# An encoder layer on one core: the first Fourier half by a written order, with its arithmetic off GpSimd and one tile in another buffer

## The chip, the cores and the metric

The kernel runs on one core of a Trainium2 chip. The core has a matrix engine (TensorE, PE in the profile, with PEld for its weight loads), a vector engine (VectorE, DVE), a scalar engine (ScalarE, ACT), a general engine (GpSimd, POOL) and a queue that mostly issues transfers (SyncE, SP). The metric is the device time of one execution in microseconds; less is better. Where runs are compared, the median of several executions is used.

## The reference

Two sequences of 1024 rows by 1024 channels (the prompt, b = 0, and the sample, b = 1) go through the same layer. Cut to what matters:

```
xn = rmsnorm(x, g_pre);  p = xn @ w_in          # 8 sections of 1024 columns
fv, fg, hv, hg, mg = split(p)
fz  = real(fft over the sequence and over groups of 256 channels of fv)
y_f = (fz * silu(fg)) @ w_fourier_out
hv  = short_conv(hv, w_short);  v, x1, x2 = split(hv)
kf  = rfft of filters made by a small network (two sines, one exponential decay)
z   = v;  for gate in (x1, x2): z = gate * long_conv(z, kf[n])     # FFT of length 2048
y_h = (z * silu(hg)) @ w_hyena_out
out = (sigmoid * y_f + sigmoid * y_h) @ w_out
y   = x + rmsnorm(out, g_post)
```

Everything is float32 in and out. Products are done on numbers split into a rounded high part and a remainder (h and l), three products for each: h by h, h by l, l by h. `split` is a rounding copy on ScalarE and a subtraction elsewhere.

## The kernel before, in words

Four stages follow one another: the Fourier branch (`phase_fourier`, to about 262 us), the filters' spectra together with some of the gate projections (the first loop of `phase_main`, to about 690 us), the long convolutions with their projections (`branches`), and the output products (`phase_tail`).

In the Fourier stage each sequence is transposed to channels by rows, scaled by `g_pre` and folded: row a is added to and subtracted from row 1024 - a, so that an even part (e = 0) and an odd part (e = 1) of half the length remain (`eo`, split to `eh` and `el`). The weights of the section `fv` are folded in the same manner (`wes` and `wos`, split to `we` and `wo`), in two halves of the channel groups. The products of the folded rows and folded weights are the sums `pfv[e, m]`, with m = 0 to 3: eight sums over eight blocks k of 128 channels. `keep` splits them to `ee` and `oo`; `fourier_half` transforms them along the sequence (`stage`: `pse`, `pso`) and along the channels (`pP`, `pQ`) and stores the result. Beside the sums there is a small product for the middle row, `pfx`, from `x5`.

The first sequence's first weight half is done by `first_half`, which works on the eight row blocks in two halves h (blocks 0, 7, 1, 6 and blocks 2, 5, 3, 4) so that work can begin when four blocks have been loaded. `scale_rows` squares the four blocks on ScalarE, gets the inverse root by a bit trick and three Newton steps of three small VectorE operations each (`rstd`), and scales the blocks, two on each engine. `two_tiles` takes two channel blocks (a pair kp): eight transposes into PSUM (`tpx`), two scaled copies to `xg` on ScalarE, a store of each to DRAM (`d_x`), two folds on VectorE, a rounding on ScalarE, a remainder on VectorE. `two_weights` loads and folds the weights of a pair; the remainder of `wo` is GpSimd's in all pairs but the first. All four pairs of h = 0 are done first, with four sums open in PSUM, then those four are kept, then come the four pairs of h = 1 with another four sums.

`hidden(0)` is the first layer of the filter network: one product, range reduction in `sin_of` on VectorE, a sine on ScalarE, a store. In later Fourier work GpSimd folds the odd part in `xtile` (the second sequence) and does one fold and one remainder for each block in `weights`.

No order is written out by hand in this stage: the framework schedules each engine's instructions by program priority in a simulated timeline, with a few edges (`issue_after`) that hold one instruction behind another on its engine. Buffers of one tag in a pool share a number of slots; a tile takes a free one, and waits if there is none.

In `filter_spectrum` the folded taps are added and subtracted to `xp` (tag `q`, two slots) and `xm` (tag `u`, one slot), then go through `butterfly` (`bs`, `b`, split to `bh` and `bl`) to the products `pXf`. The tag `u` is also that of `v`, the emptied first projection of the first branch step (`conv`, section 1). The tag `q` also holds `hid`, the network's output, which all filters' taps read. The projections (`pin`) have two PSUM pairs.

Of the kernel before, what the change touches and what calls it, by code (L numbers as in the profile page):

```python
# [9 lines left out]
F32 = mybir.dt.float32  # L10
# [6 lines left out]
P = 128  # L17
D = 1024
# [4 lines left out]
BANDS = 16  # L23

# [136 lines left out]
class K:  # L161
# [96 lines left out]
    def sin_of(self, y, k, out, src_ps, f, b):  # L258
# [12 lines left out]
        pi = 3.1415925  # L271
        nc.vector.tensor_scalar(y, y, pi, -pi, op0=ALU.min, op1=ALU.max)
        nc.scalar.activation(out, y, AF.Sin)

    def hidden(self, layer, px, pf):


        nc, a = self.nc, self.a
        h = px.tile([P, 512], F32, tag="eo", name=f"hd_{layer}", bufs=2)
        z = px.tile([P, L], F32, tag="x", name="hd_z", bufs=3)[:, 0:512]  # L280
        if layer == 0:
            w = pf.tile([P, P], F32, tag="sst", name="hd_w", bufs=1)[0:66]
            self.hfb = px.tile([P, 4], F32, name="hd_fb", bufs=1)
            z = z[0:66]
# [3 lines left out]
            y, k = [pf.tile([P, 512], F32, tag=f"{t}p0", name=f"s{t}", bufs=1 + (t == "p")) for t in "qp"]  # L288
# [7 lines left out]
        nc.tensor.matmul(p, w, z, start=True, stop=True)  # L296
        self.sin_of(y, k, h, p, self.hfb[:, 2 * layer:2 * layer + 1], self.hfb[:, 2 * layer + 1:2 * layer + 2])
        nc.sync.dma_start(self.d_h if layer else self.d_h1, h)
# [33 lines left out]
    def scale_rows(self, h, px, ss, rs):  # L332

        nc = self.nc
        q = slice(4 * h, 4 * h + 4)
        for j, m in enumerate(self.ROWS[h]):
            sq = px.tile([P, D], F32, tag="xg", name="sq", bufs=2)
            nc.scalar.activation(sq, self.xs[m], AF.Square, accum_out=ss[:, 4 * h + j:4 * h + j + 1])
        self.rstd(px, rs[:, q], ss[:, q], 4)
        for j, m in enumerate(self.ROWS[h]):  # L340
            s = rs[:, 4 * h + j:4 * h + j + 1]
            if j % 2:
                nc.scalar.mul(self.xs[m], self.xs[m], s)
            else:
                self.scaled = nc.vector.tensor_scalar(self.xs[m], self.xs[m], s, None, op0=MUL)

    def two_tiles(self, h, kp, px, fo):


        nc = self.nc  # L350
        ks = slice(2 * kp, 2 * kp + 2)
        xg = px.tile([P, 2, 514], F32, tag="xg", name=f"xg0_{h}{kp}", bufs=2)
        self.cleared = nc.gpsimd.memset(xg[:, :, 512 + h:514], 0.0)
        if h:
            nc.scalar.copy(xg[:, :, 512:513], fo["r6"][:, ks].unsqueeze(2))
        for j in range(2):
            k = 2 * kp + j
            tp = self.psum("T", 2, "tpx")
            for q, m in enumerate(sorted(self.ROWS[h])):
                nc.tensor.transpose(tp[:, q * P:(q + 1) * P], self.xs[m][:, k * P:(k + 1) * P], self.ident)  # L360
            nc.scalar.activation(xg[:, j, 0:512], tp, AF.Copy, scale=self.gpre[:, k:k + 1])
            d = self.d_x[0][k].rearrange("p (a b) -> p a b", b=256)
            self.stored = nc.sync.dma_start(d[:, 1:3] if h else d[:, 0::3], xg[:, j, 0:512].rearrange("p (a b) -> p a b", a=2))

        nc.scalar.copy(fo["r5" if h else "r6"][:, ks].unsqueeze(2), xg[:, :, 256:257])
        if h and kp == 3:
            r5 = fo["r5"].unsqueeze(2).to_broadcast([P, 8, 2])
            self.split(fo["x5"][:, :, 0:33:32], fo["x5"][:, :, 2:35:32], r5, "dve", "act")
        eo = px.tile([P, 2, 2, 2, P], F32, tag="eo", name="eo", bufs=2)
        fw = xg[:, :, 0:256].rearrange("p k (a r) -> p k r a", r=2)  # L370
        bw = xg[:, :, 512:256:-1].rearrange("p k (a r) -> p k r a", r=2)
        self.add("dve", eo[:, :, 0], fw, bw)
        self.sub("dve", eo[:, :, 1], fw, bw)
        s = slice(P * h, P * h + P)
        f = lambda t: t.rearrange("p k e r a -> p (k e r) a")
        self.split(f(fo["eh"][:, ks, :, :, s]), f(fo["el"][:, ks, :, :, s]), f(eo), "dve", "act")

    def two_weights(self, px, pw, pf, W, kp):
        nc = self.nc
        we = px.tile([P, 2, 260], F32, tag="dg", name="wes", bufs=1)  # L380
        wo = pf.tile([P, 2, 256], F32, tag=f"qp{1 - kp % 2}", name="wos", bufs=1)
        g = lambda t: t.rearrange("p (a b) -> p a b", a=2)
        for j in range(2):
            k = 2 * kp + j
            w = pw.tile([P, 2, 2, 130], F32, tag="wfv", name="wfv", bufs=2)
            nc.sync.dma_start(w.rearrange("p a b c -> p (a b c)"), self.a["w_fv"][k * P:(k + 1) * P, 0])
            self.add("dve", g(we[:, j]), w[:, :, 0], w[:, :, 1])
            self.sub("dve", g(wo[:, j]), w[:, :, 0, 0:P], w[:, :, 1, 0:P])
        for i, r in enumerate((we, wo)):
            self.split(*[p[:, 2 * kp:2 * kp + 2] for p in W[i]], r, "pool" if kp and i else "dve", "act")  # L390

    def first_half(self, pw, W, fo, px, pf, later):

        tc = self.tc
        self.xs = {}
        ss = px.tile([P, 8], F32, tag="ss", name="ss0")
        self.rs = rs = px.tile([P, 8], F32, tag="rs", name="rs0")
        self.load_rows(0, px, pf)
        self.two_weights(px, pw, pf, W, 0)
        self.load_rows(1, px, pf)  # L400
        self.scale_rows(0, px, ss, rs)
        scaled, made = self.scaled, None
        for h in range(2):
            if h:
                made = self.operands(pf)
                for e in range(2):
                    for m in (0, 2):
                        self.keep(made, e, m, p[e, m])
            p = {(e, m): self.psum(*(("X", 2) if h and e == 0 else ("mm", 4)), f"pfv{e}") for e in range(2) for m in (h, 2 + h)}
            for kp in range(4):  # L410
                if h == 0 and kp:
                    with tc.issue_after(scaled.ins):
                        self.two_weights(px, pw, pf, W, kp)
                with tc.issue_after(self.scaled.ins) if h + kp else ExitStack():
                    self.two_tiles(h, kp, px, fo)

                with tc.issue_after(self.cleared.ins):
                    for t, src in later[4 * h + kp]:
                        self.nc.gpsimd.dma_start(t, src)
                if h + kp == 0:  # L420
                    self.scale_rows(1, px, ss, rs)
                for k in (2 * kp, 2 * kp + 1):
                    for (e, m), q in p.items():
                        self.pfv(q, e, m, k, W, fo)
        return made, p

    def xtile(self, b, k, px, fo):
# [18 lines left out]
        self.sub("pool", eo[:, 1], fw, bw)  # L446
# [11 lines left out]
    def weights(self, pw, W, half, k):  # L458
# [143 lines left out]
    def phase_fourier(self):  # L602
        tc, nc, a = self.tc, self.nc, self.a
        with ExitStack() as es:
# [18 lines left out]
            for t in [fo[n] for n in ("x5", "x5t", "xx", "px")] + fo["ex"]:  # L623
                if len(t.shape) > 2:
                    t = t.rearrange("p a b -> p (a b)")
                nc.vector.tensor_scalar(t, self.ident[:, 0:1].to_broadcast(list(t.shape)), 0.0, None, op0=MUL)
# [7 lines left out]
            for b in range(NB):  # L634
# [3 lines left out]
                if b == 0:  # L638
                    self.hidden(0, px, pf)
                    W = self.open_weights(pw)  # L640
                    made, begun = self.first_half(pw, W, fo, px, pf, later)
# [5 lines left out]
                for half in ((0, 1), (1, 0))[b]:  # L647
                    if b + half not in (0, 2):
                        W = self.open_weights(pw)
                        for k in range(8):  # L650
                            self.weights(pw, W, half, k)
# [3 lines left out]
                    if (b, half) == (1, 1):  # L655
                        self.hidden(1, px, pf)
# [117 lines left out]
    def filter_spectrum(self, n, ct, T, ws):  # L774
# [7 lines left out]
        xm = ws.tile([P, 2, 4, P], F32, tag="u", name="xm", bufs=1)  # L782
# [938 lines left out]
```

## Time and profile before

| | us |
|---|---|
| median of three runs | 2364.76 (2364.63 to 2366.9) |
| the profiled execution | 2366.49 |
| its span in the trace | 2364.7 |
| TensorE busy | 2322.0 |
| VectorE busy | 1968.6 |
| ScalarE busy | 1117.0 |
| GpSimd busy | 449.8 |

A row of the busy time by stretch has the stretch, its length, then for each engine its busy time and, in brackets, its instructions (PE, PEld, DVE, ACT, POOL), then the granted clock of TensorE as a share of full speed, the busy share of the DMA engines and GB/s. A row of the timeline has the start, the duration, the engine, the line, the operation, what it writes and reads, shapes, and how many were merged (x4); in square brackets stands how long its engine was idle before it, and what ended the wait. A row of a group has the line, the engine, the operation, the tiles, the shapes and the count, then the busy time in us and the mean duration in ns, then the idle time before. Matmuls overlap: the duration of one contains its way through the array, and the step from one to the next is shorter. The helper lines are L171 (rounding copy), L177 (scalar_tensor_tensor), L181 (tensor_tensor) and L194 (matmul).

### The profile page before, as it was taken

Reading aid. Unit: us, or ns where it says so; the run is one execution under the profiler, and the core shown is the slowest. Engines: PE = TensorE matmul, PEld = TensorE weight load, DVE = VectorE, ACT = ScalarE, POOL = GpSimd, SP = SyncE. Lnnn points to the kernel's source line nnn. Section 1 sums busy time; section 2 is a strip of 40 time slices with the busy share of each in tenths; the row PEclk is TensorE's granted clock in tenths of the full one; section 3 lists DMA queues with packets and bytes.
Section 4 is the critical chain, followed back from the end, with each engine's and each line's share of the span. In section 5 each row is a group of like instructions: output and inputs, shape, how many; then the busy total and the mean of one; then the engine's idle time right before and its main releaser. Section 6 shows DMA issues by size and latency. Waiting matters only on the chain.

```text
span 2364.7 us, 36212 instructions
## 1 busy us (share of the span) xinstructions
PE 2322.0 (98%) x12784; PEld 2019.3 (85%) x12784; DVE 1968.6 (83%) x3438; ACT 1117.0 (47%) x2080; POOL 449.8 (19%) x428
## 2 busy tenths in 40 slices
PE   6999999999999999999999999999999999999998
PEld 5999888888888888888888889888888888888787
DVE  7775688888788999999989989997765578777987
ACT  6654576777753333334222223323443364557443
POOL 3342222122223343321000000112000000101311
PEclk9999999999999999999999999999999999999999
DMA  7636765554565667667465554445854678998653
GB/s 263 210 141 215 267 211 177 180 168 155 183 219 201 194 207 216 207 198 248 165 205 167 175 171 157 159 152 194 313 167 146 218 260 269 271 312 245 199 165 142
DMA packets 246207, 479.69 MB, mean 203 GB/s; under 512 B 24582, under 2 KB 82280, under 8 KB 245706
## 3 DMA queue, kind: packets, MB, share of 16 engines
q1 hardware_dynamic: 222013, 402.25, 50.9%
q0 software_dynamic: 23792, 75.11, 11.2%
q8 instruction: 100, 1.64, 0.3%
q14 instruction: 81, 0.66, 0.1%
q10 hardware_dynamic: 221, 0.04, 0.0%
HBM read 326.82 MB, written 177.73 MB: 213 GB/s over the span
## 4 chain that ended last, share of the span: by engine, by line
PE 55%; DVE 2%; DMA 1%; ACT 1%; issue 1%; POOL 0%; DVEq 0%; POOLq 0%; ACTq 0%; SPq 0%
PE pin L194 18%; PE pg L194 15%; PE pn L194 12%; PE pT L194 5%; PE pX L194 5%; PE tph L906 1%; DMA x<-d_x 1%; DMA xr<-in_x 0%; DMA d_m<-gt 0%; DMA k<-d_k 0%; DVE x L177 0%; DVE wl L181 0%; DVE t L181 0%; DVE wraw L181 0%; ACT room L171 0%
## 5 line engine op out<-in xcount | busy, mean ns | idle before, releaser
L194 PE MATMUL pin<-x,wh 128*128 128x512 f32 x2816 | 891.5, 392 | 0.6 <-DVE x L177 0.6
L194 PEld LDWEIGHTS pin<-x,wh 128*128 128x128 f32 x2816 | 525.3, 189 | 100.7 <-ACT v L873 0.8
L194 PE MATMUL pin<-x,wl 128*128 128x512 f32 x1408 | 552.1, 392 | 0.0
L181 POOL TENSOR_TENSOR wl<-wr,wh 128x512 fp32r<-128x512 f32 x128 | 224.6, 1755 | 709.7 <-ACT wh L171 682.0
L194 PEld LDWEIGHTS pin<-x,wl 128*128 128x128 f32 x1408 | 265.6, 189 | 50.0
L194 PE MATMUL pn<-room,wh 128*128 128x512 f32 x864 | 266.1, 389 | 0.0
L194 PEld LDWEIGHTS pn<-room,wh 128*128 128x128 f32 x864 | 162.1, 188 | 33.6 <-DVE gt L181 0.2
L194 PE MATMUL pn<-room,wl 128*128 128x512 f32 x432 | 168.4, 390 | 0.1
L181 DVE TENSOR_TENSOR t<-pX,k 128x1024 f32<-128x1024 f32 x128 | 156.2, 1220 | 8.7 <-PE pX L194 7.4
L194 PE MATMUL pX<-bh,cfwd 128*128 128x256 f32 x768 | 161.3, 288 | 0.0
L194 PE MATMUL pT<-cinv,yh 128*128 128x256 f32 x768 | 145.4, 284 | 0.5 <-DVE T0s L181 0.5
L171 ACT CAST wh<-wr 128x512 fp32r<-128x512 f32 x128 | 79.3, 619 | 132.7 <-PE pin L194 96.5
L171 ACT CAST bh<-b 128x512 fp32r<-128x512 f32 x144 | 88.7, 620 | 96.2 <-DVE b L181 65.5
L1362 POOL DMA_DIRECT2D d_m<-gt x32 | 27.2, 849 | 532.8 <-DVE gt L181 505.8
L194 PEld LDWEIGHTS pT<-cinv,yh 128*128 128x128 f32 x768 | 122.8, 191 | 6.5 <-issue 0.6
L194 PEld LDWEIGHTS pX<-bh,cfwd 128*128 128x128 f32 x768 | 126.3, 190 | 2.2
L171 ACT CAST yh<-y 128x512 fp32r<-128x512 f32 x96 | 59.4, 619 | 117.7 <-DVE y L181 117.7
L194 PE MATMUL pX<-bl,cfwd 128*128 128x256 f32 x384 | 109.2, 284 | 0.0
L194 PE MATMUL pT<-cinv,yl 128*128 128x256 f32 x384 | 108.9, 284 | 0.0
L181 DVE TENSOR_TENSOR bl<-b,bh 128x512 fp32r<-128x512 f32 x144 | 101.5, 709 | 3.4 <-ACT bh L171 3.3
L1105 POOL CAST mark<-x 128x1 fp32r<-128x1 f32 x30 | 22.8, 759 | 404.2 <-DVE x L177 404.0
L907 ACT COPY xt<-tph 128x512 f32<-128x512 f32 x64 | 36.9, 587 | 128.7 <-PE tph L906 128.6
(362 smaller groups left out, 5235.8 us busy)
## 6 DMA issues: line engine op xcount, KB each, us to landing
k<-d_k SPq DMA_DIRECT2D x128, 512.0 KB, 4.2
wr<-in_w_in SPq DMA_DIRECT2D x128, 256.0 KB, 3.3
d_g<-gt SPq DMA_DIRECT2D x124, 256.0 KB, 2.9
wl<-d_s SPq DMA_DIRECT2D x56, 512.0 KB, 5.5
d_k<-kt SPq DMA_DIRECT2D x128, 128.0 KB, 2.2
d_k<-kt SPq DMA_DIRECT2D x64, 256.0 KB, 2.5
g<-d_g SPq DMA_DIRECT2D x64, 256.0 KB, 5.2
r<-d_g SPq DMA_DIRECT2D x60, 256.0 KB, 6.0
```

Of the source, the lines that this page charges most:

```text
L171: self.rounded = nc.scalar.copy(h, src)
L181: return e.tensor_tensor(out, a, b, op=op)
L194: return self.nc.tensor.matmul(out, lhsT, rhs, start=start, stop=stop, skip_group_check=shared)
L906: nc.tensor.transpose(tp[:, q * P:(q + 1) * P], eo[:, e, q], self.ident)
L907: nc.scalar.copy(xt[:, e].rearrange("p a b -> p (a b)"), tp)
L1105: with tc.issue_after(nc.gpsimd.tensor_copy(mark, z[:, 0:1]).ins):
L1362: nc.gpsimd.dma_start(dst, t, accum_op=ADD)
```

## The change

There are four parts.

1. `first_half` is written out as one order. `in_order` links each instruction that it issues on TensorE, VectorE, ScalarE and SyncE behind the one before it on that engine; other instructions may still stand between. The pairs of both halves are interleaved, from (h, kp) = (0,0), (0,1), (0,2), (1,0), (1,1), (0,3), (1,2), (1,3). All eight sums are open at once: the four even ones in four banks, the four odd ones two by two in two banks. The high products of a pair are issued before those with the rows' remainder. The inverse root is a square root on ScalarE, a reciprocal and one Newton step; three of the eight squares go to VectorE; scaling is done in halves of 512 columns. The second weight pair is loaded early, into free row buffers. The remainders of `wo` are VectorE's. `keep` of m = 0 and 2 comes after the last product. Fourteen matmuls of the identity by itself stand before the first products.
2. `hidden(0)` gets twenty such matmuls behind its product, and its sine and store are issued at the end of `first_half`. The zeroing of some tiles reads `ones` (set on the core) in place of the loaded identity. The weights of the second half are held behind the remainder of (0,3) on VectorE.
3. In `xtile` and `weights` the odd fold and the remainder move from GpSimd to VectorE.
4. In the last filter, `xm` takes the tag `q` with two slots in place of `u`.

```diff
+    def in_order(self):
+        traced = self.nc.cur_bb.bb.instructions
+        last = traced[-1]
+        yield
...
+                if i.engine in prev:
+                    self.tc.add_manual_dep(i, prev[i.engine].name, ...NoSync...)
...
-        nc.scalar.activation(out, y, AF.Sin)
...
+        if layer == 0:
+            warm = self.psum("X", 2, "warm")
+            for _ in range(WARM):
+                nc.tensor.matmul(warm[:, 0:P], self.ident, self.ident, start=True, stop=True)
...
+        def norms(h):
+            q = slice(4 * h, 4 * h + 4)
+            nc.scalar.activation(root[:, q], ss[:, q], AF.Sqrt, bias=eps, scale=1.0 / D)
+            nc.vector.tensor_scalar(low[:, q], ss[:, q], -0.5 / D, -0.5 * RMS_EPS, op0=MUL, op1=ADD)
+            nc.vector.reciprocal(rs[:, q], root[:, q])
+            self.mul("dve", sq4[:, q], rs[:, q], rs[:, q])
+            self.mul("dve", sq4[:, q], sq4[:, q], low[:, q])
+            self.stt("dve", rs[:, q], sq4[:, q], 1.5, rs[:, q], ADD, MUL)
...
+        with self.in_order():
+            nc.scalar.activation(root[:, 0:1], self.ones[:, 0:1], AF.Sqrt)
+            for j in range(4):
+                square(0, j, "act" if j < 3 else "dve")
+            norms(0); scale(0, 0)
...
+            sumsof(0); sumsof(1); trans(0, 0); scale(0, 1); sums(0); load_w(2)
+            evac(0, 0); cast(0); trans(0, 1); fold(0, 0); high(0, 0); evac(0, 1)
+            lows(0); rest(0, 0); warm(14); products(0, 0)
+            sums(1); cast(1); square(1, 0, "act"); fold(0, 1); trans(0, 2); high(0, 1)
+            evac(0, 2); lows(1); rest(0, 1); products(0, 1)
+            square(1, 1, "act"); square(1, 2, "dve"); square(1, 3, "dve")
+            sums(2); load_w(3); norms(1); scale(1, 0); trans(1, 0); fold(0, 2); cast(2)
+            high(0, 2); evac(1, 0); trans(1, 1); lows(2); rest(0, 2); products(0, 2)
+            fold(1, 0); evac(1, 1); sums(3); high(1, 0); cast(3); fold(1, 1); scale(1, 1)
+            trans(0, 3); rest(1, 0); products(1, 0); evac(0, 3); high(1, 1); lows(3)
+            fold(0, 3); trans(1, 2); rest(1, 1); products(1, 1); evac(1, 2); high(0, 3)
+            fold(1, 2); trans(1, 3); rest(0, 3)
+            self.opened = self.left
+            products(0, 3); evac(1, 3); high(1, 2); fold(1, 3); rest(1, 2)
+            products(1, 2); high(1, 3); rest(1, 3)
...
+            products(1, 3)
...
+            sine()
...
-        self.sub("pool", eo[:, 1], fw, bw)
+        self.sub("dve", eo[:, 1], fw, bw)
...
-        self.sub("pool", wo, w[:, :, 0, 0:128], w[:, :, 1, 0:128])
+        self.sub("dve", wo, w[:, :, 0, 0:128], w[:, :, 1, 0:128])
...
-            self.split(t[0][:, k], t[1][:, k], r.rearrange("p a b -> p (a b)"), "pool" if r is wo else "dve", "act")
+            self.split(t[0][:, k], t[1][:, k], r.rearrange("p a b -> p (a b)"), "dve", "act")
...
-                        for k in range(8):
-                            self.weights(pw, W, half, k)
+                        with tc.issue_after(self.opened.ins) if b == 0 else ExitStack():
+                            for k in range(8):
+                                self.weights(pw, W, half, k)
...
-        xm = ws.tile([P, 2, 4, P], F32, tag="u", name="xm", bufs=1)
+        last = (n, ct) == (1, 7)
+        xm = ws.tile([P, 2, 4, P], F32, tag="q" if last else "u", name="xm", bufs=1 + last)
```

The steps are written several to a line here. `square`, `scale`, `trans`, `evac`, `fold`, `high` and `rest` are one step each of the rows' way: the square, the scaling of a half of 512 columns, eight transposes, two copies out of PSUM with their stores, two folds, the rounding, the remainder. `sums`, `cast` and `lows` are the weights' folds, roundings and remainders. `products` is a pair's 24 products (two parts, two sums each, two blocks k, three products): 16 with the rows' rounded part, then 8 with their remainder.

More of the change, by code (lines that the diff above doesn't have):

```diff
@@ L287, in hidden @@
             nc.scalar.dma_start(self.hfb, a["filt_fb"])
-            y, k = [pf.tile([P, 512], F32, tag=f"{t}p0", name=f"s{t}", bufs=1 + (t == "p")) for t in "qp"]
-        else:
+            y, k = [pf.tile([P, 514], F32, tag="pp0", name=f"s{t}", bufs=2)[:, 0:512] for t in "yk"]
+            h = y
+        else:
+            h = px.tile([P, 512], F32, tag="eo", name="hd_1", bufs=2)
+            z = px.tile([P, L], F32, tag="x", name="hd_z", bufs=3)[:, 0:512]
             nc.sync.dma_start(z, self.d_h1)
@@ L375, in two_tiles @@
[L375 to L425, printed above, removed]
@@ L638, in phase_fourier @@
                 if b == 0:
-                    self.hidden(0, px, pf)
+                    sine = self.hidden(0, px, pf)
                     W = self.open_weights(pw)
-                    made, begun = self.first_half(pw, W, fo, px, pf, later)
+                    made, begun = self.first_half(pw, W, fo, px, pf, later, sine)
                 else:
```

254 lines of the change are left out of this document (210 added, 44 removed).

## The prediction

> **What bounds the kernel now.** I read the page's busy shares first, then the busy time by stretch, then the waits, and last the timeline of the two stretches in which TensorE idles.
>
> ```profile
> PE 2322.0 (98%) x12784; PEld 2019.3 (85%) x12784; DVE 1968.6 (83%) x3438; ACT 1117.0 (47%) x2080; POOL 449.8 (19%) x428
> ```
> ```profile
> 0.00:60.00 60.00, 38.17 (x259) 33.81 (x260) 44.43 (x91) 41.44 (x73) 18.32 (x31) 1.00 0.80 264
> 60.00:262.00 202.00, 198.02 (x1430) 185.42 (x1429) 132.57 (x311) 107.38 (x242) 65.52 (x73) 1.00 0.56 193
> 120.00:140.00 20.00, 17.23 (x143) 16.61 (x142) 19.60 (x26) 13.91 (x32) 10.05 (x11) 1.00 0.66 249
> 676.00:680.00 4.00, 2.86 (x16) 2.14 (x14) 4.00 (x12) 2.54 (x6) 0.14 (x1) 1.00 0.33 85
> 680.00:684.00 4.00, 2.45 (x11) 2.48 (x12) 4.00 (x9) 1.95 (x6) 2.16 (x3) 0.61 0.98 286
> 684.00:688.00 4.00, 3.43 (x14) 2.97 (x13) 4.00 (x8) 3.57 (x7) 0.00 (x0) 0.50 0.45 172
> 688.00:692.00 4.00, 4.00 (x12) 3.11 (x12) 4.00 (x10) 1.35 (x4) 0.00 (x0) 0.61 0.28 95
> ```
>
> TensorE is the bound: 2322.0 of 2364.7 us busy, so at most 42.7 us of its idle time, plus what it loses at half clock, can be won. Of that idle time 21.8 us lie in the first 60 us (60.00 less 38.17), 4.0 us in the rest of the Fourier stage (202.00 less 198.02), and 3.3 us at 676 to 688, where the granted clock also falls to 0.50. These are the three places that the change touches.
>
> **The change: the beginning.** Its working is a walk through the hand-written order, engine by engine, each instruction starting when its engine is free and its inputs are there.
>
> ```profile
> 3.99 2.05 PE L296 MATMUL phd<-hd_z,hd_w 66*128 66x512 f32 x2 [3.99 <-DMA hd_z<-in_c_z]
> 10.52 1.06 ACT L338 ACTIVATE sq<-x 128x1024 f32<-128x1024 f32 x1
> 11.40 0.43 DVE L272 TENSOR_SCALAR sq<-sq 128x512 f32<-128x512 f32 x1
> 13.36 0.16 DVE L253 SCALAR_TENSOR_TENSOR rs_t<-rs 128x4 f32<-128x4 f32 x1
> 16.62 1.42 DVE L345 TENSOR_SCALAR x<-x,rs 128x1024 f32<-128x1024 f32 x2
> 19.00 1.11 PE L360 MATMUL tpx<-ident,x 128*128 128x128 f32 x4 [0.22 <-ACT x L343]
> 25.47 1.22 PE L194 MATMUL pfv<-we,eh 128*128 128x260 f32 x4
> 30.30 2.19 ACT L343 ACTIVATE x<-x,rs 128x1024 f32<-128x1024 f32 x2 [1.88 <-DVE rs L255]
> 34.05 0.75 PE L194 MATMUL pfv<-we,eh 128*128 128x260 f32 x4 [3.02 <-ACT eh L171]
> 35.11 1.03 PE L360 MATMUL tpx<-ident,x 128*128 128x128 f32 x8
> 55.16 0.52 PE L194 MATMUL pse<-seq,ee 128*128 128x258 f32 x3
> 57.43 0.52 PE L194 MATMUL pso<-seq,ee 128*128 128x258 f32 x3
> 57.78 2.07 PE L194 MATMUL pfx<-we,x 128*36 128x260 f32 x16
> 62.45 0.28 PE L194 MATMUL pfv<-wo,el 128*128 128x256 f32 x1
> ```
> ```profile
> L181 DVE TENSOR_TENSOR eo<-xg 128x512 f32<-128x512 f32 x16 | 10.2, 687 | 0.3 <-ACT xg L361 0.3
> L181 DVE TENSOR_TENSOR el<-eo,eh 128x1024 fp32r<-128x1024 f32 x8 | 10.1, 1276 | 3.0 <-ACT eh L171 2.9
> L181 DVE TENSOR_TENSOR wes<-wfv 128x260 f32<-128x260 f32 x8 | 3.3, 424 | 0.0
> L181 DVE TENSOR_TENSOR we<-wes,we 128x520 fp32r<-128x520 f32 x4 | 2.8, 695 | 0.4 <-ACT we L171 0.4
> ```
> ```profile
> L361 ACT ACTIVATE xg<-tpx,gpre 128x512 f32<-128x512 f32 x16 | 10.5, 685 | 0.2 <-PE tpx L360 0.2
> L171 ACT CAST eh<-eo 128x1024 fp32r<-128x1024 f32 x8 | 8.4, 1046 | 2.1 <-DVE eo L181 2.1
> ```
>
> *Opening.* The fourth row is there when its square starts at 10.52; that does not move. VectorE now squares it (about 1.25 us by the 1276 ns row, the nearest of that size), while the sine's preparation, which follows the matmul that ends at 6.04 and ended at 11.8 (11.40 and 0.43), should be over by then: the zeroing ahead of it no longer waits for the identity. The sine itself goes to the end, where ScalarE is some 3 us ahead of TensorE, with its table load. So the squares are in at 11.8. One square root on ScalarE and five small operations (13.36: 0.16, about 0.2 with the handing on) replace eleven: the scale is ready at 13.2; before, scaling began at 16.62. Scaling in halves (0.37 us each on VectorE, 0.6 on ScalarE, half of the rows 16.62 and 30.30) starts the transposes at 14.5, about 3 us earlier. ScalarE does its second scaling halves before it empties the transposes, so the first fold starts at 17.4. The twenty warming matmuls cost nothing: they run from 6.0 to 11.6 at the slow rate of row 19.00 (0.28 each), and TensorE has no input before 14.5; without that cover they would cost 5.6. The fourteen later ones (3.9 at that rate) hold the first products back by some 2.2 us, hidden by TensorE's wait for the second rows, below.
>
> *Middle.* From 17.4 VectorE is the bound: 16 folds 10.2, eight remainders 9.6 (1.2 undisturbed), eight weight remainders 5.2 (three of them come from GpSimd), twelve weight sums 5.0, two squares 2.5, second scaling and norm 2.5: 35.0 us, with 2 us of waits done at 54. On the way, the second rows are scaled only at 33.4 (fold, remainders, sums of two pairs and two squares stand before it: 17.4 + 14.8, then 1.2 on ScalarE), and the transposes of the next pair wait for PSUM behind a cast, a rounding and an emptying on ScalarE (1.2 + 1.05 + 1.7) until about 36.5 to 37.
>
> *End.* From 36.5 TensorE has no more gap: eight transpose groups of 0.52 (35.11: 0.13 each) and six sets of 24 products at 0.12 (57.78): 4.2 + 17.3, end at 58.0. Before, the same products end at 62.6 with 22 other matmuls between them (55.16, 57.43, 57.78), 2.6 us: 60.0 without. The gain is 2.0 at best and not the 3 of the opening, because VectorE's work in the middle is hardly less.
>
> Against it stands the clock. TensorE idles from 31.0 to 36.5 but for two transpose groups. Row 34.05 says a gap of 3.02 us in this place leaves the rate whole (0.12 a step); the stretch at 680 says a gap of 2.7 halves it. If it halves here, the products run from 36.5 to about 42 at half rate, and the same walk ends at 60.9 to 61.9: 0.9 to 1.9 us worse than before. I take +0.5, between the two, since the gap is longer than the harmless one but split; ends +2.0 and -1.9. After the products sixteen x5 products cover the roundings of the sums, which before were half done earlier.
>
> [...]
>
> *Queues.* SP's order is fixed by hand too: the second weight pair is loaded into row buffers behind the rows, the sine's store moves to the end, where nothing waits for it, and each store of an emptied tile must land before its buffer's second reuse.
>
> ```profile
> DMA to landing us min/median/max: 2.2/3.8/7.8
> ```
>
> At 3.8 no reuse waits (the shortest interval is 5 us); at 7.8 throughout the walk ends 4 us later. The table loads on GpSimd's queue follow the new order and are not needed before 60.
>
> **Fourier arithmetic off GpSimd.**
>
> ```profile
> 23.30 1.58 POOL L181 TENSOR_TENSOR wo<-wos,wo 128x512 fp32r<-128x512 f32 x1 [1.54 <-ACT wo L171]
> 23.67 1.23 DVE L254 SCALAR_TENSOR_TENSOR rs_t<-rs_t,rs_m 128x4 f32<-128x4 f32 x1
> ```
> ```profile
> L181 POOL TENSOR_TENSOR wo<-wor,wo 128x256 fp32r<-128x256 f32 x16 | 15.8, 1000 | 25.0 <-ACT wo L171 24.7
> L181 POOL TENSOR_TENSOR eo<-xg 128x512 f32<-128x512 f32 x8 | 14.1, 1765 | 11.0 <-ACT xg L440 5.3 <-DVE el L181 2.5 <-ACT x L451 1.9
> L181 POOL TENSOR_TENSOR wor<-wfv 128x256 f32<-128x256 f32 x16 | 13.0, 821 | 4.1 <-DMA wfv<-in_w_fv 3.8 <-DVE sst L547 0.3
> ```
> ```profile
> L181 DVE TENSOR_TENSOR el<-eo,eh 128x1024 fp32r<-128x1024 f32 x8 | 12.3, 1550 | 0.0
> L181 DVE TENSOR_TENSOR eo<-xg 128x512 f32<-128x512 f32 x8 | 8.7, 1090 | 0.4
> L181 DVE TENSOR_TENSOR we<-wer,we 128x260 fp32r<-128x260 f32 x16 | 8.7, 565 | 0.1
> ```
>
> VectorE takes 32 operations of 0.42 and 8 of 0.69: 19 us more. It gets back what GpSimd's presence cost it: a 4-column operation took 1.23 us beside GpSimd (23.67) and 0.16 without (13.36). In the later stretch remainders take 1550 ns against 1.2, folds 1090 against 687, weight remainders 565 against 424: 8 x 0.35 + 8 x 0.40 + 16 x 0.14 = 8.3 to be had back. Net +11 us on 132.6 of 202: hidden by TensorE's backlog, except at 120 to 140 where VectorE is full (19.60 of 20.00); there 8 x 0.69 = 5.5 come and 6.0 go. The gain is at most TensorE's idle 4.0, the loss at most the 11. I take +0.5: TensorE is busy 98% here, so nearest to nothing. Half 1's weight work now follows the last fold's remainder; before, it could start only when the first weights' buffer came free, which is unchanged.
>
> **The last filter's xm.** The first branch tile v takes the single buffer that xm holds.
>
> ```profile
> 681.55 1.19 PE L194 MATMUL pXf<-b,cfw 128*128 128x128 f32 x4 [2.69 <-ACT bs L691]
> 685.09 1.11 ACT L873 ACTIVATE v<-pin,wsh 128x1024 f32<-128x1024 f32 x1
> 691.58 0.62 PE L194 MATMUL pin<-x,wh 128*128 128x512 f32 x2
> ```
>
> v's emptying stands at 685.09, behind the last reader of xm, so its PSUM pair stays full, no next projection can start, and TensorE idles 2.69 us and 0.57 more, then runs slow until 691.58: 2.45 x 0.39 + 3.43 x 0.50 + 4.00 x 0.39 = 4.2 lost by the clock rows. Together 7.5 us are to be had, and nothing if VectorE, full in all four windows, doesn't finish v's two passes sooner. What is late next is VectorE itself and the next projection's weights. I take 4, the middle: the buffer of the filter's input features is free by then, so the emptying surely comes early, and the slow stretch shortens even if the gap stays.
>
> **Sum.** 0.5 + 0.5 + 4 = 5 us. The profiled execution took 2366.5 (span 2364.7), 1.7 above the median 2364.76; from the median the sum gives 2359.8.
>
> **Rivals.**
> 1. *Nothing reaches TensorE at 680*: v's passes find no room before 682 in VectorE's queue. For it: VectorE at 4.00 of 4.00. Against it: ScalarE is idle 6.6 of those 16 us, so v can be emptied once its products are done. Gain 1: 2363.8.
> 2. *All of it comes*: clock whole at 36 (2.0), the full 7.5, and 2 of the Fourier gaps: 11.5, 2353.3. For it: row 34.05. Against it: all three must hold.
> 3. *The clock falls at 31 to 36* and the last products run at half rate to about 42: -1.4 instead of +0.5 in the beginning, 2361.7. For it: the 0.50 at 684 after 2.7 us of waiting. Against it: row 34.05. [...]
> 4. *Slower: VectorE becomes the bound of the Fourier stage.* Should the long VectorE operations not be GpSimd's doing, the 5.5 us come on a full engine at 120 to 140, and at 60 to 80, where half 1's weights fall (16 x 0.42 = 6.6), a further 3.6 exceed its room, estimated at 3.0: 9.1 on the path. Less the 5: 2368.9. It decides as soon as more than 5 us of the 9.1 reach TensorE. For it: 19.60 of 20.00. Against it: the pair 23.30 and 23.67.
>
> **How the numbers follow.** 0.2% is 4.7 us, about what a measurement here can tell from no change. Forecast 0.36 (most of it just beyond 0.2%), rival 2 0.16, rival 1 0.18, rival 3 0.14, rival 4 0.16. Rival 2 and two thirds or more of the forecast (with what replanning of the later stages adds) are faster: 0.46; rivals 1 and 3 and the rest of the forecast the same: 0.38; rival 4 slower: 0.16. Range: 2350.0 (rival 2 and 3 us of replanned gaps, from the 13.6 us of idle time outside the three places) to 2369.0 (rival 4).
>
> **What would show it.** Right: first transposes near 14.5, first products before 23, last of them by 58 to 61 with VectorE busy throughout; no product row of 0.24 a step after 36; GpSimd's share down by the 43 us of its three groups and the 1550 ns remainders back at 1.2; v emptied before 675 and the clock windows of 0.50 at 680 gone or shorter. Wrong: gaps in TensorE at 60 to 140 released by VectorE; or the 2.69 us wait unchanged.

## The result, and the profile after

The changed kernel took 2354.72 us (median; 2351.06 to 2356.71) against 2364.95 (2362.66 to 2366.9) on the same chips: ratio 0.9956, 95% interval [0.9945, 0.9966], so 10.2 us faster by the medians. The profiled execution took 2355.18, its span is 2353.4.

The busy shares of the changed kernel, and its busy time by stretch (columns as in the prediction):

```profile
PE 2323.0 (99%) x12852; PEld 2024.6 (86%) x12852; DVE 1973.4 (84%) x3479; ACT 1107.4 (47%) x2073; POOL 409.3 (17%) x386
```
```profile
0.00:60.00 60.00, 48.97 (x354) 45.62 (x355) 49.35 (x107) 43.00 (x84) 8.42 (x27) 0.94 0.83 278
60.00:262.00 202.00, 198.17 (x1419) 186.34 (x1418) 138.74 (x347) 108.34 (x238) 26.77 (x36) 0.99 0.57 198
120.00:140.00 20.00, 20.00 (x170) 19.82 (x169) 18.10 (x37) 14.40 (x33) 1.26 (x4) 1.00 0.48 177
676.00:680.00 4.00, 4.00 (x23) 3.43 (x22) 4.00 (x9) 1.81 (x6) 3.35 (x3) 1.00 0.30 87
680.00:684.00 4.00, 4.00 (x28) 3.64 (x28) 4.00 (x7) 2.44 (x6) 2.31 (x3) 1.00 0.53 188
684.00:688.00 4.00, 4.00 (x21) 3.35 (x20) 4.00 (x14) 2.58 (x7) 0.00 (x0) 1.00 0.54 191
688.00:692.00 4.00, 4.00 (x22) 3.38 (x21) 2.70 (x8) 2.33 (x5) 2.33 (x3) 1.00 0.49 146
```

TensorE's idle time is 30.4 us where it was 42.7. At 680 it has no gap and the whole clock. At 120 to 140 its gaps are gone, and yet the Fourier stage as a whole idles as much as before (202.00 less 198.17): a new gap stands at 112 to 116. The waits of TensorE name it (waited for, total, times, longest); rows of the two other engines' timelines follow the same moment:

```profile
PE phd L315 <- DMA hd_w<-in_filt_w: 3.7, 1, 3.7
PE tpx L426 <- issue: 3.2, 1, 3.2
PE pse L195 <- ACT sev L698: 2.5, 1, 2.5
```
```profile
113.06 0.69 ACT L597 ACTIVATE xg<-tpx,gpre 128x512 f32<-128x512 f32 x1 [2.77 <-DMA d_x<-xg]
...
115.17 0.36 ACT L698 COPY sev<-pse 34x258 f32<-34x258 f32 x1
```
```profile
115.58 1.27 PE L195 MATMUL pse<-seq,oo 128*128 128x258 f32 x6 [2.47 <-ACT sev L698]
116.64 3.31 PE L195 MATMUL tpx<-dg,xk 128*128 128x128 f32 x16
...
122.79 1.95 PE L195 MATMUL tpx<-dg,xk 128*128 128x128 f32 x16
```

ScalarE waits 2.77 us for a store of `xg` to land before it may use that buffer again; the copy `sev` is queued behind it on ScalarE, and TensorE waits 2.47 us for the copy. Then the next sixteen products `tpx` take 3.31 us instead of 1.95: the granted clock is 0.50 from 116.1 to 119.5. All runs with the written order and the arithmetic off GpSimd have this wait for `sev` (1.8 to 2.5 us), the others don't.

Start times of the same instruction in both profiles tell where the time went. The 62.7 us of before are set to 60.1, without the 2.6 us of other matmuls that stood between the products.

| | before | after | difference |
|---|---|---|---|
| last products of the first half end | 60.1 | 56.9 | -3.2 |
| last `pQ` (end of the Fourier stage) | 240.8 | 236.9 | -3.9 |
| first `pn` | 270.5 | 264.2 | -6.3 |
| first `pX` of the branches | 715.3 | 703.2 | -12.1 |
| last `pX` | 1620.7 | 1609.9 | -10.8 |
| last `pg` of the tail | 2357.0 | 2345.7 | -11.3 |

So some 3 us come from the beginning, 8 from the filters' stage, and nothing from the later ones. Read from this trace alone, the 8 would be put down to xm. The experiments say otherwise.

### The profile page after: what moved, and what is told of

Same layout as the page of the kernel before. It is cut to its first block, busy times and chain, and to the rows that moved or that the text cites. A ratio compares the mean times of both kernels' runs of the same rounds, so it can differ in the third digit from the quotient of the medians.

```text
span 2353.4 us, 36339 instructions
## 1 busy us (share of the span) xinstructions
PE 2323.0 (99%) x12852; PEld 2024.6 (86%) x12852; DVE 1973.4 (84%) x3479; ACT 1107.4 (47%) x2073; POOL 409.3 (17%) x386
## 4 chain that ended last, share of the span: by engine, by line
PE 56%; DVE 2%; DMA 1%; issue 1%; ACT 0%; POOL 0%; DVEq 0%; SPq 0%; POOLq 0%; ACTq 0%
PE pin L195 19%; PE pg L195 15%; PE pn L195 12%; PE pT L195 5%; PE pX L195 5%; PE tph L1065 1%; DMA xr<-in_x 0%; DMA d_m<-gt 0%; DVE wl L182 0%; DMA oB<-d_wo 0%; DVE room L182 0%; DVE wraw L182 0%; DVE o L182 0%; DVE gt L182 0%; DVE x L178 0%
## 5 line engine op out<-in xcount | busy, mean ns | idle before, releaser
L182 POOL TENSOR_TENSOR wl<-wr,wh 128x512 fp32r<-128x512 f32 x128 | 237.4, 1855 | 715.1 <-ACT wh L172 684.9
L182 DVE TENSOR_TENSOR t<-pX,k 128x1024 f32<-128x1024 f32 x128 | 155.8, 1217 | 10.4 <-DMA k<-d_k 5.4
L195 PEld LDWEIGHTS pn<-room,wl 128*128 128x128 f32 x432 | 81.1, 188 | 17.4 <-DVE wl L182 0.5
```

The lines of the kernel that those rows point to most:

```text
L182: return e.tensor_tensor(out, a, b, op=op)
L195: return self.nc.tensor.matmul(out, lhsT, rhs, start=start, stop=stop, skip_group_check=shared)
```

## Experiments: the three edits, alone and in pairs

Theory A was that the edits add up: 3 us from the written order, up to 3 from VectorE freed of GpSimd, 5 to 8 from xm. Rivals were that the gains come of the later stages being planned anew, and that VectorE becomes the bound. "The order" below is parts 1 and 2 of the change together.

**xm alone.**

```diff
 (the kernel before)
-        xm = ws.tile([P, 2, 4, P], F32, tag="u", name="xm", bufs=1)
+        last = (n, ct) == (1, 7)
+        xm = ws.tile([P, 2, 4, P], F32, tag="q" if last else "u", name="xm", bufs=1 + last)
```


> The kernel before, with the last filter's xm in the tag q and nothing else. Theory A (the tile is the cause of the waits at 680): v is emptied about 20 us earlier than at 685, TensorE's idle 2.69 and 0.57 us and the slow clock behind them go, the time falls by 5 to 8 us. Rival B (the gap at 680 went because everything stood earlier and was planned anew): the waits there stay, the time moves by less than 2 us. Rival C: the gap goes, but the 2 us waits and slow clock at 268 to 276 stay, so the time falls by the 7.5 us of 680 alone, to about 2357.

Ratio 1.0032 [1.0019, 1.0044]: slower by 7.6 us, which no theory had foreseen.

**Arithmetic off GpSimd alone.**

```diff
 (the kernel before)
-        self.sub("pool", eo[:, 1], fw, bw)
+        self.sub("dve", eo[:, 1], fw, bw)
...
-        self.sub("pool", wo, w[:, :, 0, 0:128], w[:, :, 1, 0:128])
+        self.sub("dve", wo, w[:, :, 0, 0:128], w[:, :, 1, 0:128])
...
-  "pool" if r is wo else "dve", "act")
+  "dve", "act")
```


> The kernel before, with the odd folds and the remainders of the second sequence and of the later weights on VectorE in place of GpSimd, nothing else. Theory A: VectorE's operations get shorter by about what it takes over (el back from 1550 to 1200 ns), TensorE's 2.8 us of gaps at 120 to 140 go: 0 to -3 us. Rival (VectorE becomes the bound there): gaps released by VectorE at 60 to 140, +3 to +9 us.

Ratio 0.9981 [0.9972, 0.9989]: 4.5 us, a little more than theory A had, and no loss.

**The order alone.**

```diff
 (the changed kernel)
-  "dve" (the three places above)
+  "pool"
...
-        xm = ws.tile([P, 2, 4, P], F32, tag="q" if last else "u", name="xm", bufs=1 + last)
+        xm = ws.tile([P, 2, 4, P], F32, tag="u", name="xm", bufs=1)
```


> The changed kernel with the Fourier arithmetic put back on GpSimd and xm back in its old tag: the written order, the late sine and the warming matmuls stand alone. Theory A: the last products of the first half end near 57 as in the changed kernel, so -3 us against before, and the waits at 680 are back. Rival B (the later stages are planned better because the beginning is shorter): -6 us or more, with the waits at 680 or at 270 gone.

Ratio 1.0016 [1.0007, 1.0025]: slower, although the last products end at 57.4, near the changed kernel's 56.9.

**Without xm.** The changed kernel with the last two lines of that diff.

> The changed kernel with xm back in its old tag. Theory A: the waits at 680 are back, so the time stands 5 to 8 us above the changed kernel, about 3 to 5 below the kernel before. Rival B (the waits at 680 went through the earlier start): within 2 us of the changed kernel.

Ratio 0.9969 [0.9961, 0.9978]: 3.1 us above the changed kernel, less than the 5 to 8 of theory A, and no more than the noise of such a difference, so this run alone does not rule out rival B. The traces point to theory A: at 676 to 692 TensorE idles 1.1 us again, and the first `pX` starts at 705.8 where the changed kernel has 703.2.

**GpSimd back.** The changed kernel with "pool" in the three places, xm kept in `q`.

> The changed kernel with the Fourier stage's later arithmetic back on GpSimd (the written order and xm stay). Theory A (the beginning's 3 us reach the end of the stage only when VectorE's operations are freed of GpSimd): the last pQ stands 2 us behind the kernel before as with the order alone, waits of TensorE on VectorE at 60 to 262 sum to 8 us or more; the time is 3 to 6 us above the changed kernel. Rival (the parts add up): the loss against the changed kernel is no more than the 4.5 us that the part wins alone, and the beginning's 3 us are still there at the last pQ.

Ratio 1.0053 [1.004, 1.0066]: 23 us behind the changed kernel, where 3 to 6 were expected. Neither theory had it.

**Off GpSimd and xm, without the order.** The kernel before with the diffs of the first two runs.

> The kernel before with the arithmetic off GpSimd and the last filter's xm in the tag q, without the written order. Theory A (the 8 us that the xm change lost alone come from another drawing of the order in the branches and not from the buffer): waits at 1300 to 1550 are gone, and the time is 7 to 11 us below before, the written order adds less than 3 us to these two. Rival (the buffer in q is itself what delays the branches): 8 us of waits at 1300 to 1550, time about 3 us above before.

Ratio 0.9958 [0.9945, 0.997]: as theory A had it. The two small edits give nearly the whole gain.

With the kernels before and after, every combination has been run. In microseconds against before (the ratio less one, times 2366; each good to some 2 to 3 us, so a difference of two to 3 or 4):

| | neither | off GpSimd | xm | both |
|---|---|---|---|---|
| old order | 0 | -4.5 | +7.6 | -9.9 |
| written order | +3.8 | -7.3 | +12.5 | -10.4 |

The edits don't add up. Taking the arithmetic off GpSimd wins in every row. The written order loses 4 to 5 us without it, wins 2.8 beside it, and on top of both other edits 0.5; the last two can't be told from nothing. xm loses 8 or 9 us without it and wins 3 to 5 with it. Two questions follow.

*Why does the order lose while GpSimd still works?* Busy time by stretch, of the order alone and then of the arithmetic off GpSimd alone:

```profile
60.00:262.00 202.00, 193.30 (x1397) 181.02 (x1397) 130.75 (x301) 106.12 (x233) 64.12 (x71) 1.00 0.54 185
```
```profile
60.00:262.00 202.00, 199.17 (x1444) 187.28 (x1444) 140.40 (x356) 111.42 (x247) 26.12 (x36) 1.00 0.58 198
```

TensorE arrives 3 us earlier at 57 and then idles 8.7 us until 262 (202.00 less 193.30), 4.7 more than before; the longest single wait is 2.9 us for VectorE's `qp` at 123. With the arithmetic on VectorE it idles 2.8 in the old order, and 4.0 in the written one (the run without xm, 202.00 less 197.99). The reason stands in VectorE's and GpSimd's timelines of the order alone:

```profile
121.72 2.02 DVE L182 TENSOR_TENSOR eo<-xg 128x512 f32<-128x512 f32 x1
123.66 1.99 DVE L182 TENSOR_TENSOR qp<-sst,qp 128x514 fp32r<-128x514 f32 x1
...
128.61 1.21 DVE L182 TENSOR_TENSOR el<-eo,eh 128x1024 fp32r<-128x1024 f32 x1
...
130.24 2.40 DVE L182 TENSOR_TENSOR el<-eo,eh 128x1024 fp32r<-128x1024 f32 x1
...
133.17 0.41 DVE L182 TENSOR_TENSOR fB<-pQ,fPm 128x255 f32<-128x255 f32 x1
134.28 0.94 DVE L182 TENSOR_TENSOR qp<-sst,qp 128x514 fp32r<-128x514 f32 x1
```
```profile
120.78 2.41 POOL L182 TENSOR_TENSOR eo<-xg 128x512 f32<-128x512 f32 x1 [2.67 <-DVE sst L704]
...
123.36 1.74 POOL L182 TENSOR_TENSOR eo<-xg 128x512 f32<-128x512 f32 x1
...
130.00 1.55 POOL L182 TENSOR_TENSOR eo<-xg 128x512 f32<-128x512 f32 x1 [2.52 <-DVE el L182]
132.81 1.85 POOL L182 TENSOR_TENSOR eo<-xg 128x512 f32<-128x512 f32 x1 [1.26 <-DVE el L182]
```

The same subtraction took 1.21 us at 128.61 and 2.40 at 130.24, where it began while GpSimd subtracted: GpSimd ended at 131.55, and 1.21 more is 132.76, within 0.2 of its end at 132.64. The `qp` of 134.28 was late in the same way (GpSimd ended at 134.66, plus its usual 0.68 is 135.34; it ended at 135.22). `fB` at 133.17, inside GpSimd's operation of 132.81, took its usual 0.41. So not every operation of VectorE took longer beside GpSimd; which do, and why, no run tests. The first two rows of each show what this did to the longest wait: the fold at 121.72 took 2.02 us and the `qp` at 123.66 took 1.99, each about 0.68 by itself, so 2.6 of TensorE's 2.9 us are what these two took beyond that.

*Why does xm lose without the other edit?* Busy time at 1200 to 1610, of the kernel before and then of xm alone, and the waits of xm alone there:

```profile
1200.00:1610.00 410.00, 410.00 (x2456) 364.99 (x2454) 380.58 (x630) 121.43 (x223) 41.74 (x40) 1.00 0.53 167
```
```profile
1200.00:1610.00 410.00, 401.72 (x2397) 356.11 (x2396) 375.48 (x619) 118.78 (x217) 37.28 (x39) 0.99 0.54 164
```
```profile
PE tph L907 <- ACT T1s L960: 2.8, 2, 2.0
PE pT L194 <- ACT yh L171: 1.5, 2, 1.2
PE pX L194 <- DVE bl L181: 1.4, 3, 1.0
PE pX L194 <- DVE t L181: 1.4, 1, 1.4
```

At 680 xm does what it was meant to do: `v` is emptied at 663.5, and 676 to 692 has no gap. But 600 us later, in the branches, in which the edit changes no work, TensorE idles 8.3 us, on waits for ScalarE and VectorE that before did not have. Order and xm without the other edit idles 8.6 us there, on the same waits. In both programs TensorE's list in the branches is another than before's, and the same in the two: projections (`pin`) stand elsewhere between the transforms. In the other twelve programs of this document (before itself among them) the list is before's, as far as the traces record it, from 746 us of before to the end, and none of them idles more than 0.5 us there. The framework plans all stages in one simulated run, so an edit at 680 can draw another order for 1300. Why that order makes TensorE wait is not shown.

## Experiments: is it the buffer or the order?

Sixteen small loads of `hyena_d`, moved to another queue, happen to give xm alone the kernel before's list in the branches. The same line was put into the kernels before and after as controls.

```diff
-        nc.sync.dma_start(db, a["hyena_d"][n, ct].partition_broadcast(P))
+        nc.gpsimd.dma_start(db, a["hyena_d"][n, ct].partition_broadcast(P))
```


> xm in the tag q and nothing else of the change (GpSimd keeps its Fourier arithmetic), with one neutral edit: the small loads of hyena_d are issued on GpSimd's queue and not on SP's. With it the framework's order of TensorE in the branches is the kernel before's again over the last 4976 products, where xm alone had another. Theory A (xm alone lost its 8 us through that other order, not through the buffer): no waits on T1s, yh or bl at 1300 to 1550, the waits at 680 are gone, and the time is 3 to 6 us below the kernel before. Rival (the buffer does it): the 8 us of waits at 1300 to 1550 come again, the time is 5 to 8 us above before.

> The kernel before with the neutral edit alone (the loads of hyena_d on GpSimd's queue). Control for the run of xm with that edit: all theories expect within 1.5 us of before. Should it move by more, the edit itself is not neutral, and that run has to be read against this one.

> The changed kernel with the neutral edit alone; TensorE's order in the branches is the changed kernel's to the last product. Expected: within 2 us of the changed kernel, so a ratio of 0.995 to 0.9965. More than that says how much of any few us here is drawing and not cause.

Ratios: xm with this line 1.0006 [0.9997, 1.0015], before with it 1.0026 [1.0015, 1.0037], after with it 0.9943 [0.993, 0.9955]. The time of the first is above what theory A had (3 to 6 us below before). The second is outside what was expected: the line is not neutral. It costs before 6.2 us; the 3.1 that it gains on after are more than expected too, but no more than the noise. Read against its own control, as was set down for that case, xm wins 4.7 us, and its waits in the branches are gone. Busy time by stretch of xm with the line, then of before with the line:

```profile
676.00:692.00 16.00, 16.00 (x91) 13.93 (x91) 15.89 (x35) 6.85 (x14) 6.80 (x8) 1.00 0.59 190
1200.00:1610.00 410.00, 409.82 (x2454) 364.88 (x2453) 380.01 (x630) 121.78 (x224) 41.51 (x40) 1.00 0.56 168
```
```profile
676.00:692.00 16.00, 13.05 (x76) 11.42 (x75) 15.59 (x33) 9.20 (x18) 5.75 (x7) 0.99 0.67 227
1200.00:1610.00 410.00, 409.69 (x2456) 364.84 (x2455) 379.94 (x630) 121.26 (x221) 41.31 (x40) 1.00 0.56 168
```

The buffer is worth 4.5 us at the first `pX` (715.0 against 719.5), and the branches follow at about the same distance (4.2 at the last). So xm alone lost through the order that was drawn with it, not through its buffer. For part 3 this isn't settled to the same degree: its 17 to 23 us beside xm hold those 8 us of another drawing, and only its 4.5 alone and its 11.1 beside the order are free of them.

## Experiments: the clock and the fillers in the beginning

```diff
 (the changed kernel; "no warming")
-WARM = 20
+WARM = 0
...
-            warm(14)
```


> The changed kernel without the twenty and the fourteen warming matmuls. Theory A (an idle TensorE comes to its first transposes cold, and the clock comes back within about 1.3 us of work): first transposes and the first products at 0.24 to 0.29 a step, the products then begin up to 2 us earlier but the last of them end no earlier, because VectorE sets the pace: 0 to +2 us. Rival (without the warming the whole beginning stays slow to 36): the last products end 2 to 4 us later, at 59 to 61.

```diff
 (the changed kernel; "filled gap")
+            spin(12)        # identity by itself, into the bank of p[0, 1]
             trans(1, 0)
```


> The changed kernel with twelve more matmuls of the identity by itself, issued on TensorE between the second pair's products and the second rows' first transposes, into a bank that no sum has begun. They fill the idle 3.2 us at 28 to 31. Theory A (idleness lets the clock fall at 31, and the slow transposes and products up to 37.5 cost about 2 us): the transposes there take 0.12 each, not 0.29, and the last products end 1 to 2 us before 56.7. Rival (VectorE's next operands set the pace anyway): the transposes are fast, the last products end within 0.5 us of 56.7.

Both edits together:

> The changed kernel without its thirty-four warming matmuls and with the twelve in the gap at 28 to 31. Theory A (neither reaches the end of the first half, since VectorE and ScalarE pace it): last products at 56 to 57, and the time between the runs without warming and with the filled gap, ratio 0.994 to 0.9955. Rival (the filled gap is what won 4 us over the changed kernel): ratio 0.993 to 0.994 again.

Ratios: no warming 0.995 [0.9936, 0.9963], filled gap 0.9938 [0.9926, 0.9951], both 0.9955 [0.9942, 0.9967]. Last products end at 56.6, 57.1 and 57.1 (0.5 us of other matmuls stand between in the latter two), the changed kernel's at 56.9. TensorE's timeline of the changed kernel, then of the filled gap, then of no warming:

```profile
31.19 2.34 PE L426 MATMUL tpx<-ident,x 128*128 128x128 f32 x8 [3.21 <-issue]
34.65 1.97 PE L426 MATMUL tpx<-ident,x 128*128 128x128 f32 x8 [1.12 <-ACT xg L435]
36.27 1.80 PE L195 MATMUL pfv<-we,eh 128*128 128x260 f32 x8
37.91 1.11 PE L195 MATMUL pfv<-wo,eh 128*128 128x256 f32 x8
...
39.82 1.04 PE L426 MATMUL tpx<-ident,x 128*128 128x128 f32 x8
...
56.26 0.63 PE L195 MATMUL pfv<-wo,el 128*128 128x256 f32 x4
```
```profile
27.33 2.84 PE L490 MATMUL pfv<-ident 128*128 128x128 f32 x24
...
31.51 0.87 PE L426 MATMUL tpx<-ident,x 128*128 128x128 f32 x6 [0.28 <-ACT x L419]
34.18 1.88 PE L426 MATMUL tpx<-ident,x 128*128 128x128 f32 x8 [1.79 <-ACT xg L435]
35.71 2.08 PE L195 MATMUL pfv<-we,eh 128*128 128x260 f32 x8
```
```profile
13.48 2.39 PE L426 MATMUL tpx<-ident,x 128*128 128x128 f32 x8 [7.71 <-DMA x<-in_x]
16.13 1.97 PE L426 MATMUL tpx<-ident,x 128*128 128x128 f32 x8 [0.26 <-ACT xg L435]
19.18 2.10 PE L195 MATMUL pfv<-we,eh 128*128 128x260 f32 x8 [1.08 <-ACT eh L456]
...
23.62 0.64 PE L195 MATMUL pfv<-wo,el 128*128 128x256 f32 x4
```

Without warming TensorE is slow for far longer than the 1.3 us of work that theory A had: the first eight products, at 19.18, take 2.10 us where the changed kernel's at 20.43 take 1.20, and only the four at 23.62 take 0.64 as there. The end does not move: TensorE's rate there does not set it. With the gap filled the next transposes are fast (0.87 for six), but the granted clock, 1.00 at 31 to 34, is 0.58 at 34 to 36 all the same, and the end does not move either, as the rival had it. The filled gap's 4 us against the changed kernel therefore do not come from the first half. The last `pQ` does stand 2.0 us earlier with it (234.9), but 2.7 earlier with both edits (234.2), where the 4 us are not there. 2350.64 us is the lowest median here, 14.7 below before by its ratio, and no cause of it has been shown: its interval and the changed kernel's overlap, and the profiled execution was the slowest of its five (2356.98), so its trace can't tell.

## Why the prediction was right or wrong

The time was inside the range and the direction right; the gain was 10.2 where 5 were forecast. It came out near rival 2's time (2353.3), and that is luck: of rival 2's three conditions the clock was not whole at 36, xm did not bring the full 7.5, and the gaps at 120 to 140 went, but one of the same size came at 113. What the sum had wrong is above all the second term, the arithmetic off GpSimd, as said below.

- **Opening: right.** The scale was ready at 13.1 (forecast 13.2). First transposes at 13.67 (forecast 14.5), first products at 20.43 (forecast before 23). The warming costs nothing, as worked out, and brings nothing.
- **End of the first half: 1.1 us too late.** The sets of products were to run from 36.5; they ran from 36.27. "Eight transpose groups" were counted as still to come, 4.2 us; of these only 24 transposes stood behind the first products (39.82 and two more rows like it, 0.8 each), 2.4 us. That is 1.8 less, and the slow clock took 0.6 (the first set took 3.55 us, the next 2.93): 58.0 becomes 56.8, and 56.9 was measured.
- **The clock (rival 3): fell as it said, and cost 0.6 us, not 3 to 4.** It was whole again at 37.6 (0.60 over 36 to 38), not at 42. The 0.50 at 31 to 36 was right; the price assumed that it must be waited out during products, and TensorE went idle at 28.0 and not at 31.0, so most of the slow stretch fell on gaps and transposes. (The price is itself loose: 5.5 us at half rate lose 2.75, which gives 60.8; how 61.9 comes about isn't said.) The row 34.05, on which the choice between rivals 2 and 3 rested, was an exception. All five runs that keep the beginning of before have a wait of 3.57 or 3.58 us in its place with a slow clock behind it (in the run of before with the moved loads it is 0.94 over the first 60 us, in before 1.00); this is that row with xm alone, its four products in 1.23 us where row 34.05 has 0.75:

```profile
34.21 1.23 PE L194 MATMUL pfv<-we,eh 128*128 128x260 f32 x4 [3.58 <-ACT eh L171]
```

One profile of before could not show this. There too the fall cost little: in the three of them that are before's program up to 60, the last products end 0.3 to 0.7 us after 62.7.
- **Beginning as a whole: +0.5 forecast, 3.2 at its end, about 0.5 in the time (to some 3 us).** The step "no reuse waits" held in the first half, for which it was worked out; nothing was worked out for the second sequence's blocks, and there, at 113, a store lands late (the DMA share is 1.01 to 1.03 at 110 to 116; that this load delays it is a guess and was not tried). 2.5 us of waiting and 3.4 us at a clock of 0.50 took most of the gain back. So the +0.5 agrees by luck: the prediction had the clock eat the gain in the first half. At the last `pQ` the changed kernel stands at 236.9, and the kernel without the written order but with both other edits at 237.6.
- **Fourier arithmetic off GpSimd: +0.5 forecast, 4.5 alone.** "Net +11 us" on VectorE was 7.8 (140.40 against 132.57), since its unlisted folds of `wer` came back too (569 to 422 ns). The wrong step is "at most TensorE's idle 4.0": the wait of 2.1 us at 270 and the clock of 0.50 behind it (271.2 to 274.7), in the filters' stage, go as well (first `pn` 4.9 us earlier in that run, 2.5 of them there at the last `pQ` already; VectorE ends the sum `acc`, for which `pn` waits, at 265.1, and at 270.4 in before), and the order's gain cannot reach the end without it. Rival 4 was wrong: TensorE's waits for VectorE at 60 to 262 sum to 1.8 us before and to 1.1 in that run. (Its 16 x 0.42 is 6.7 and not 6.6, which changes nothing.) GpSimd lost 38.8 of 65.5 us at 60 to 262, and the remainders came back to 1.2 as forecast:

```profile
L182 DVE TENSOR_TENSOR el<-eo,eh 128x1024 fp32r<-128x1024 f32 x8 | 9.7, 1218 | 2.7 <-ACT eh L172 2.7
...
L182 DVE TENSOR_TENSOR we<-wer,we 128x260 fp32r<-128x260 f32 x16 | 6.6, 425 | 0.1
```

- **xm: +4 forecast, 3.1 in place** (5.4 beside part 3 alone, 4.7 against its control; each to 3 or 4): right in size, as far as that goes. `v` is emptied at 661.56, before 675 as stated, and rival 1 fell. The full 7.5 did not come, because without xm the changed kernel's gap at 676 to 692 had already shrunk from 3.3 to 1.1 us through the other edits.
- **What was missing altogether** is a term for the order that the framework draws anew. The prediction allowed 3 us of gain for it. The runs show +6.2 us on before (and -3.1, within the noise, on after) for one line that moves sixteen loads, and 8 us of new waits 600 us behind the edit.

## What to carry to other kernels

Where a framework plans the order of the whole program, judge an edit by what it does to its own stage and by the list of instructions behind it, and run it with a control that changes no work: a few microseconds either way may be another drawing. An edit that pays only when another engine is freed looks like a loss when it is tried alone, so try combinations before throwing a part away. Arithmetic moved to GpSimd to relieve VectorE can take VectorE's time anyway: in the rows shown here one subtraction of VectorE took 2.40 us where it began beside GpSimd's and 1.21 by itself. And a rate that one profile shows in one place may be another in the next execution of the same instructions: four products at 34 took 0.75 us in one profile and 1.23 in another.

## What the runs showed of the hardware

- In the profile of before the granted clock was 0.50 from 271.2 to 274.7 and from 680.8 to 691.1, in that of after from 30.8 to 37.6 and from 116.1 to 119.5 (and in both for the last 5 us of the span). The waits of TensorE there were 2.10 us (before, 270.52), 2.69 (before, 681.55), 3.21 (after, 31.19) and 2.47 (after, 115.58), the slow stretches 3.4, 10.2, 6.8 and 3.4 us: the longest wait does not have the longest of them.
- The waits of 3.02 us (before, 34.05) and of 2.94 us (the order alone, 125.71) had no such stretch: the clock reads 1.00 over 31 to 40 and over 122 to 126. So in these profiles the length of the wait alone does not tell whether the rate falls, and what does was not shown. The fall at 271.2 in before cost the wait of 2.1 us and, as an estimate from 3.4 us at 0.50, 1.7 more.
- The same instructions can meet another rate. The run of before with the moved loads has before's beginning, and its first products start at 25.47 in both; the first four took 0.94 us in that run (the first row below) and 1.22 in before, where two products still took 0.53 at 28.63 and then 0.40 at 29.00.
- The column of the granted clock does not show this slow beginning: in before it reads 1.00 at 24 to 28, where those four products took 1.22 us (four took 0.75 at 34.05), and without warming 1.00 at 16 to 20, where the eight transposes of 16.13 took 1.97 (eight took 1.04 at 39.82 in the changed kernel). In the beginning the steps have to be read.
- What transposes do to the rate is not settled by these runs. Without warming, sixteen of them from 13.48 to 18.1 stayed at 0.25 to 0.30 us each, and the first products behind them, at 19.18, took 0.26 each. With the gap filled, the last fillers end at 30.2, the transposes at 31.51 follow at the full rate (0.87 for six), and the eight at 34.18 took 1.88. In the changed kernel, between its fillers' end at 12.47 and 17.38, TensorE ran sixteen transposes and nothing else, and the next fillers still came at 0.11 a step, as the last of those before had (the last three rows).

```profile
25.47 0.94 PE L194 MATMUL pfv<-we,eh 128*128 128x260 f32 x4
```
```profile
5.58 6.89 PE L319 MATMUL warm<-ident 128*128 128x128 f32 x40
...
16.32 1.23 PE L426 MATMUL tpx<-ident,x 128*128 128x128 f32 x8 [0.93 <-ACT xg L435]
17.38 3.29 PE L195 MATMUL pfv<-ident 128*128 128x128 f32 x28
```
